# p.v of an attention layer in unsplit fp32, two key/value heads in the two column halves of TensorE

## The chip, the cores and the metric

The kernel runs on one core of one Trainium2 chip. The metric is the time of an execution on the device in microseconds; three runs of the kernel before gave a median of 988.04 us (985.65 to 988.46).

## The reference

One encoder layer is applied with shared weights to two requests: `x_prompt` of 1024 tokens and `x_sample` of 512, both 1024 wide, all in fp32. A combined projection gives a retention branch of 4 heads and an attention branch with 8 query heads of 64 columns over 2 key/value heads. The attention is bidirectional and without a mask:

```
sc  = einsum('bqkgd,bskd->bkgqs', qi, k) * scale
p   = softmax(sc, axis=-1)
out = einsum('bkgqs,bskd->bqkgd', p, v)
```

Four query heads share a key/value head. The output of each branch is gated, the branches are concatenated, and one output projection, a gate and a residual follow.

## The kernel before

The kernel runs the sample first (`sequence(1, 4, True)`, `nt` = 4 token tiles of 128) and then the prompt (`sequence(0, 8, False)`, `nt` = 8). Names of tiles end in `s` or `p` for the two. Each sequence has a part with projections and retention, and a part with the attention and the output projection, in which rows of both are mixed.

Precise products are made on TensorE from operands split into a high part, which fits fp32r, and the rest (`split`, L137): the high part by a cast on ScalarE or GpSimd, the low part by a subtraction on VectorE or GpSimd. `mm3` (L147 to L150) then takes three matmuls. A matmul of plain fp32 operands is issued once and shows in the trace as two records of weight load and two of matmul.

For a query tile t (128 queries), `nat_head` (L849) computes the scores of one query head against all keys for their maximum only (`pn`, reduced by VectorE to `nm`). `st_unit` (L900) then computes transposed scores, keys on partitions: a unit u is a head v and a pair of key blocks kp, and gives 128 keys x 512 (four query heads of 128 queries) twice in a `wide` PSUM tile `pT`. A first matmul for each block multiplies k by `Q1T`, a second one (65 rows) adds the low parts and minus the maximum, from `Q2T`, which has one buffer for each v and is filled by `mid_t` (L867). ScalarE's exp (L912) writes `p`, in fp32; `split` makes `ph` (ScalarE) and `pl` (VectorE). GpSimd adds p into `acc` (L921, L924), a slot of 512 columns for each head that all query tiles use in turn.

`pv_unit` (L926) multiplies with V. V is kept split, `VV[:, kb, v, :, :]` holding 64 columns of high part and 64 of low part, in opposite order for the two heads. With these 128 columns as weights and `ph` and `pl` as moving operands, `po` holds products with the high part in one half of its partitions and with the low part in the other; at the end of a head ScalarE copies the low half to `o` (L950) and VectorE adds the high half (L951). Units run over the key blocks of head 0 first and head 1 next, so `po` is opened and emptied twice for each query tile.

`row_sums` (L954) multiplies each head's `acc` with a 64-column block of ones, fp32, into half of the partitions of `pL`. `normalise` (L960) takes its reciprocal as exp(-ln) on ScalarE, multiplies the gate in (L969) and multiplies `o` by it (L970). `gate_out` splits the result for the output projection `out_step` (L1008), whose result `py` is scaled and added to the residual by VectorE (L1019, L1020) and stored.

PSUM has 8 banks. In the attention part of the prompt three `wide` tiles (two banks each) hold `pT`, `pn`, the transposes and `pL`, and two `bank` tiles hold `po` and `py`; in the sample there are two wide tiles and four banks.

The order is planned. Each step is put into a round with a priority by `at_round`; a tile has nt + 1 rounds, and the steps of neighbouring tiles fall into the same rounds (the maxima of the next tile, the output projection of the one before). The steps are traced in that order, and a scheduler with a simulated timeline then fixes each engine's instruction order and the buffers. On the chip an engine works its list in order. `tc.high_priority()` moves instructions ahead in the scheduler, and `add_manual_dep` adds a dependency.

Of the kernel before, what the change touches and what calls it, by code (L numbers as in the profile page):

```python
# [11 lines left out]
F32 = mybir.dt.float32  # L12
F32R = mybir.dt.float32r
BF16 = mybir.dt.bfloat16
AF = mybir.ActivationFunctionType
ALU = mybir.AluOpType
AX = mybir.AxisListType
PSUM = bass.MemoryType.PSUM

P = 128  # L20
# [18 lines left out]
KPOST = (1, 1)  # L39
PESUM = (0, 0)  # L40
EPS = 1e-6
# [37 lines left out]
def hybrid_layer_kernel(ctx: ExitStack, tc: tile.TileContext, a: dict, y_prompt: bass.AP, y_sample: bass.AP):  # L79
# [34 lines left out]
    V.memset(mhalf, -0.5)  # L114
    zo = cst.tile([P, 4, DH], F32R, name="zo")
    for i in range(4):
        V.tensor_scalar(out=zo[:, i, :], in0=ident[:, 0:DH], scalar1=0.0, scalar2=float(i == 2), op0=ALU.mult, op1=ALU.add)
    zr = zo[:, 0:2, :].rearrange("p i d -> p (i d)")
    ones = zo[:, 2, :].bitcast(F32)
    vones = [zo[:, 2 - v : 4 - v, :].rearrange("p i d -> p (i d)") for v in range(2)]  # L120

# [169 lines left out]

    def x_stats(pl, tag, x, name, sp=None):
        sp = sp or pl
        junk = pl.tile([P, D], BF16, tag=tag, name=f"junk{name}")
        ss = sp.tile([P, 1], F32, tag="xss", name=f"ss{name}", bufs=4)
        S.activation(junk, x, AF.Square, accum_out=ss)
        rr = rsqrt(sp, ss, 1, 1.0 / D, EPS, f"x{name}")
        G.tensor_scalar(out=x, in0=x, scalar1=rr, scalar2=0.0, op0=ALU.mult, op1=ALU.add)
# [16 lines left out]
    def sequence(r, nt, first):  # L315
# [4 lines left out]
        with ExitStack() as sctx:  # L320
# [18 lines left out]
            def open_kv():  # L339
                kvp = sctx.enter_context(pool(f"kv{tg}", bufs=1, reuse_waits="tile"))  # L340
                kv["k"] = [kvp.tile([P, ntok], F32R, name=f"kk{tg}{v}") for v in range(2)]
                kv["k2"] = [kvp.tile([65, ntok], F32R, name=f"k2{tg}{v}") for v in range(2)]
                kv["V"] = kvp.tile([P, nt, 2, 2, DH], F32R, name=f"VV{tg}")
                kv["g"] = kvp.tile([P, 2, DH], F32, name=f"gq{tg}")
                kv["gate"] = [kvp.tile([P, 512], F32, name=f"gate{tg}{n}") for n in range(2)] if first else gmod
# [84 lines left out]
            def kvq_units(pa):  # L430
                def kv_unit(g, tabs):
# [16 lines left out]
                    for u, pj in enumerate(pjs):  # L448
                        gs_ = slice(g * 4 + 2 * u, g * 4 + 2 * u + 2)
                        for v in range(2):  # L450
                            src = pj[:, :, P + v * DH : P + (v + 1) * DH]
                            S.copy(VV[:, gs_, v, v, :], src)
                            V.tensor_tensor(VV[:, gs_, v, 1 - v, :], src, VV[:, gs_, v, v, :].bitcast(F32), op=ALU.subtract)
                    V.tensor_tensor(t1, t1, rr.unsqueeze(2).broadcast_to([P, 8, DH]), op=ALU.mult)
# [433 lines left out]

            pesum = order[:PESUM[r]]

            def st_first(t, u):
                v, kp = u // (nt // 2), u % (nt // 2)
                hs = slice(v * 4, v * 4 + 4)
                pT = st8[t]["pT", u] = wide(f"pT{tg}{t}{u}")
                for i in range(2):
                    kb = slice((2 * kp + i) * P, (2 * kp + i + 1) * P)
                    T.matmul(pT[:, i * 512 : (i + 1) * 512], kk[v][:, kb], st8[t]["Q1T"][:, hs, :].rearrange("p h q -> p (h q)"),  # L897
                             start=True, stop=False)

            def st_unit(t, u):  # L900
                d = st8[t]
                v, kp = u // (nt // 2), u % (nt // 2)
                hs = slice(v * 4, v * 4 + 4)
                if ("pT", u) not in d:
                    st_first(t, u)
                pT = d.pop(("pT", u))
                for i in range(2):
                    kb = slice((2 * kp + i) * P, (2 * kp + i + 1) * P)
                    T.matmul(pT[:, i * 512 : (i + 1) * 512], k2[v][:, kb], d["Q2T", v],  # L909
                             start=False, stop=True)  # L910
                p = pools["at"].tile([P, 1024], F32, tag="p", name=f"p{tg}{t}{u}")
                S.activation(p, pT, AF.Exp)  # L912
                ph = pools["at"].tile([P, 1024], F32R, tag="ph", name=f"ph{tg}{t}{u}", bufs=3 if first else 2)
                pl = pools["at"].tile([P, 1024], F32R, tag="pl", name=f"pl{tg}{t}{u}", bufs=3 if first else 2)
                split(S.copy, V, ph, pl, p)
                d[u] = (ph, pl)
                acc = qs[tps[0]][:, v * 512 : (v + 1) * 512]
                if t in pesum:
                    pass
                elif kp == 0:  # L920
                    G.tensor_tensor(acc, p[:, 0:512], p[:, 512:1024], op=ALU.add)  # L921
                else:
                    for i in range(2):
                        G.tensor_tensor(acc, acc, p[:, i * 512 : (i + 1) * 512], op=ALU.add)  # L924

            def pv_unit(t, u):  # L926
                d = st8[t]
                v, kp = u // (nt // 2), u % (nt // 2)
                ph, pl = d.pop(u)
                if kp == 0:  # L930
                    d["po"] = bank(f"po{tg}{t}{v}")
                if u == 0:
                    d["o"] = pools["q2"].tile([P, 512], F32, tag="o", name=f"o{tg}{t}", bufs=3 if first else 1)
                po, o = d["po"], d["o"]
                for i in range(2):
                    kb = 2 * kp + i
                    c = slice(i * 512, (i + 1) * 512)
                    lv = VV[:, kb, v, :, :].rearrange("p a d -> p (a d)")
                    T.matmul(po, lv, ph[:, c], start=(kb == 0), stop=False)  # L939
                    T.matmul(po, lv, pl[:, c], start=False, stop=(kb == nt - 1))  # L940
                if t in pesum:
                    if u == 0:
                        d["L"] = bank(f"pL{tg}{t}")
                    for i, z in enumerate((ph, pl)):
                        for j in range(2):
                            T.matmul(d["L"], vones[v], z[:, j * 512 : (j + 1) * 512],
                                     start=(u == 0 and i + j == 0), stop=(u == nt - 1 and i + j == 2))
                if kp == nt // 2 - 1:
                    mn = slice(v * DH, (v + 1) * DH)
                    S.copy(o[mn, :], po[(1 - v) * DH : (2 - v) * DH, :])  # L950
                    V.tensor_tensor(o[mn, :], po[mn, :], o[mn, :], op=ALU.add)  # L951

            def row_sums(t):
                if t in pesum:  # L954
                    return
                pl = st8[t]["L"] = bank(f"pL{tg}{t}") if nt == 4 else wide(f"pL{tg}{t}")[:, 0:512]
                for v in range(2):
                    T.matmul(pl[v * DH : (v + 1) * DH, :], ones, qs[tps[0]][:, v * 512 : (v + 1) * 512], start=True, stop=True)  # L958

            def normalise(t):  # L960
                pl, o = st8[t]["L"], st8[t]["o"]
                with tc.issue_after(acts["ln"].ins):
                    S.activation(pl, pl, AF.Ln, scale=2.0)
                S.activation(pl, pl, AF.Exp, scale=-1.0)
                tq = slice((t % 4) * P, (t % 4 + 1) * P)
                for jj in range(2):
                    gv = gs[t // 4 * 2 + jj].rearrange("p (j q) -> p j q", j=2)[:, :, tq]
                    lv = pl[:, jj * 256 : (jj + 1) * 256].rearrange("p (j q) -> p j q", j=2)
                    V.tensor_tensor(lv, lv, gv, op=ALU.mult)  # L969
                V.tensor_tensor(o, o, pl, op=ALU.mult)  # L970

# [65 lines left out]
            for n, t in enumerate(order):  # L1037
# [4 lines left out]
                for v in range(2):  # L1042
# [3 lines left out]
                    at_round(hb + per_ - 1 if n == 0 else m, 7, lambda t=t, v=v: mid(t, v))  # L1046
                    at_round(m + 1 + (0 if first else 2 if n and v else 0), 1.5 if first and not soon or n == 0 else 3.5, lambda t=t, v=v: mid_t(t, v))
                for u in range(nt):
# [3 lines left out]
                    at_round(b + u, 3, lambda t=t, u=u: st_unit(t, u))  # L1052
                    at_round(b + u + 1, 4, lambda t=t, u=u: pv_unit(t, u))
                at_round(b + nt, 4.5, lambda t=t: row_sums(t))
# [12 lines left out]
            if first:  # L1067
# [4 lines left out]
                for t in range(NAHEAD):  # L1072
                    at_round(nt * per_ - 8 + t, 0, lambda t=t: x_load(0, t, xnext[t]))
                    at_round(nt * per_ - 5 + t, 10, lambda t=t: x_stats(pools["at"], "p", xnext[t], f"0{t}", ate))
            for j in range(8):
# [61 lines left out]
```

## Time and profile before

| | |
|---|---|
| median of 3 runs | 988.04 us (985.65 to 988.46) |
| span of the profiled execution, first to last instruction | 985.3 us |
| TensorE busy | 938.8 us, 95% |
| TensorE weight loads | 813.9 us, 83% |
| VectorE busy | 626.1 us, 64% |
| GpSimd busy | 507.7 us, 52% |
| ScalarE busy | 414.3 us, 42% |

The profiled execution has no time of its own beside its span; the median lies 2.7 us above it. In the rows, PE is TensorE's matmuls, PEld its weight loads, DVE VectorE, ACT ScalarE, POOL GpSimd; L940 is line 940 of the kernel. Matmuls overlap in their pipeline, so a row's duration is longer than the distance to the next row's start. A tile's name without its number stands for all of its kind.

### The profile page before, as it was taken

The page shows a single profiled execution, that of the slowest core. Times are in us where ns is not written, and L with a number is a line of the kernel's source. Part 1 is how long each engine was busy: PE and PEld are TensorE (multiplying, and loading weights), DVE is VectorE, ACT ScalarE, POOL GpSimd, SP SyncE. Part 2 cuts the span into 40 slices and gives each one's busy share as a digit, 9 for nine tenths or more (in the row PEclk, how much of TensorE's full clock was granted, in tenths as well). Part 3 has the DMA queues.
Part 4 walks back from the last instruction along what each step waited for, and adds up shares of the span by engine and source line. Part 5 has one row for each costly group of instructions (what it writes and reads, how often), then busy time and mean ns, then how long its engine had stood idle before and what let it go on. Part 6 is the DMA issues. An engine that isn't in the chain of part 4 may idle for free. (4 is left out here: it accounts for less than half of the span.)

```text
span 985.3 us, 15952 instructions
## 1 busy us (share of the span) xinstructions
PE 938.8 (95%) x6249; PEld 813.9 (83%) x6249; DVE 626.1 (64%) x1039; ACT 414.3 (42%) x656; POOL 507.7 (52%) x404
## 2 busy tenths in 40 slices
PE   4889998999999999999999999999979999999998
PEld 3779898987676799999999988999847776776776
DVE  2474556667886683534435243457988878978975
ACT  4252233353646652122321322241465655655562
POOL 4243544474647663122223012255899779777882
PEclk9999998999999999999999999999999999999999
DMA  9964876321911711111111112100071110111011
GB/s 274 275 191 144 269 225 218 87 78 57 382 67 44 239 50 47 41 43 44 44 35 28 26 43 70 47 7 12 1 296 68 43 44 1 44 43 45 20 43 44
DMA packets 95687, 93.02 MB, mean 94 GB/s; under 512 B 23502, under 2 KB 84858, under 8 KB 92540
## 3 DMA queue, kind: packets, MB, share of 16 engines
q1 hardware_dynamic: 92876, 77.85, 25.8%
q0 software_dynamic: 2736, 14.16, 3.6%
q8 instruction: 49, 0.80, 0.3%
q14 instruction: 26, 0.21, 0.1%
HBM read 77.30 MB, written 14.68 MB: 93 GB/s over the span
## 5 line engine op out<-in xcount | busy, mean ns | idle before, releaser
L924 POOL TENSOR_TENSOR qp<-qp,pp 128x512 f32<-128x512 f32 x96 | 159.5, 1661 | 21.3 <-ACT pp L912 15.3
L139 DVE TENSOR_TENSOR plp<-pp,php 128x1024 fp32r<-128x1024 f32 x64 | 93.6, 1464 | 19.8 <-ACT php L138 19.7
L912 ACT ACTIVATE pp<-pTp 128x1024 f32<-128x1024 f32 x64 | 65.6, 1025 | 76.8 <-PE pTp L909 40.7
L856 DVE TENSOR_REDUCE nmp<-pnp 128x1 f32<-128x1024 f32 x64 | 77.3, 1212 | 11.4 <-PE pnp L854 11.4
L138 ACT CAST php<-pp 128x1024 fp32r<-128x1024 f32 x64 | 67.2, 1051 | 16.2 <-PE pop L939 14.9
L148 PE MATMUL pvgp<-wvgp,hhp 128*128 128x256 f32 x224 | 65.1, 291 | 0.0
L148 PE MATMUL pqkp<-wqkp,hhp 128*128 128x256 f32 x224 | 64.7, 289 | 0.0
L149 PE MATMUL pvgp<-wvgp,hhp 128*128 128x256 f32 x224 | 64.4, 288 | 0.0
L150 PE MATMUL pvgp<-wvgp,hlp 128*128 128x256 f32 x224 | 63.9, 285 | 0.0
L150 PE MATMUL pqkp<-wqkp,hlp 128*128 128x256 f32 x224 | 63.7, 284 | 0.0
L149 PE MATMUL pqkp<-wqkp,hhp 128*128 128x256 f32 x224 | 63.4, 283 | 0.0
L940 PE MATMUL pop<-plp,VVp 128*128 128x512 f32 x128 | 52.1, 407 | 5.7 <-DVE plp L139 5.6
L148 PE MATMUL pyp<-wo,Mhp 128*128 128x512 f32 (+1 forms) x136 | 52.8, 389 | 1.2 <-DVE op L951 0.7
L150 PE MATMUL pyp<-wo,Mlp 128*128 128x512 f32 (+1 forms) x136 | 51.6, 382 | 0.5 <-DVE Mlp L139 0.5
L149 PE MATMUL pyp<-wo,Mhp 128*128 128x512 f32 (+1 forms) x136 | 51.9, 382 | 0.0
L639 POOL TENSOR_TENSOR sp<-rt1p,rt2p 128x512 f32<-128x512 f32 x16 | 22.5, 1405 | 56.4 <-DVE rt2p L636 56.4
L939 PE MATMUL pop<-php,VVp 128*128 128x512 f32 x128 | 51.0, 398 | 0.3 <-ACT php L138 0.3
L124 POOL TENSOR_SCALAR m_retp<-ssp 128x4 f32<-128x4 f32 x8 | 1.6, 195 | 89.6 <-DVE ssp L745 89.4
L897 PE MATMUL pTp<-Q1Tp,kkp 128*128 128x512 f32 x128 | 41.4, 404 | 3.6 <-ACT pp L912 2.9
L148 PEld LDWEIGHTS pqkp<-wqkp,hhp 128*128 128x128 f32 x224 | 43.0, 192 | 0.0
L149 PEld LDWEIGHTS pqkp<-wqkp,hhp 128*128 128x128 f32 x224 | 43.0, 192 | 0.0
L150 PEld LDWEIGHTS pqkp<-wqkp,hlp 128*128 128x128 f32 x224 | 42.9, 192 | 0.0
(465 smaller groups left out, 3120.7 us busy)
## 6 DMA issues: line engine op xcount, KB each, us to landing
wo<-wod SPq DMA_DIRECT2D x16, 1024.0 KB, 5.8
wa<-in_w_ada_dram SPq DMA_DIRECT2D x16, 512.0 KB, 6.4
wod<-woz POOLq DMA_DIRECT2D x8, 1024.0 KB, 6.0
gr<-in_w_ada_dram SPq DMA_DIRECT2D x16, 256.0 KB, 4.8
xn<-in_x_prompt_dram SPq DMA_DIRECT2D x8, 512.0 KB
xrp<-in_x_prompt_dram SPq DMA_DIRECT2D x8, 512.0 KB, 3.4
out_dram<-xrp POOLq DMA_DIRECT2D x7, 512.0 KB, 3.0
xs<-in_x_sample_dram SPq DMA_DIRECT2D x4, 512.0 KB, 6.1
```

Source lines behind the costliest of these rows:

```text
L138: hi_eng(hi, src)
L139: lo_eng.tensor_tensor(lo, src, hi.bitcast(F32), op=ALU.subtract)
L148: T.matmul(out, lh, rh, start=first, stop=False)
L149: T.matmul(out, lh, rl, start=False, stop=False)
L150: T.matmul(out, ll, rh, start=False, stop=last)
L639: G.tensor_tensor(qk, t1, t2, op=ALU.add)
L856: V.tensor_reduce(nm[:, h : h + 1], pn[:, :ntok], AX.X, ALU.max, negate=True)
L897: T.matmul(pT[:, i * 512 : (i + 1) * 512], kk[v][:, kb], st8[t]["Q1T"][:, hs, :].rearrange("p h q -> p (h q)"), start=True, stop=False)
L912: S.activation(p, pT, AF.Exp)
L924: G.tensor_tensor(acc, acc, p[:, i * 512 : (i + 1) * 512], op=ALU.add)
L939: T.matmul(po, lv, ph[:, c], start=(kb == 0), stop=False)
L940: T.matmul(po, lv, pl[:, c], start=False, stop=(kb == nt - 1))
```

## The change

V is kept once, in fp32 (`VV` of nt x 2 x 64 columns); its split goes. p is not split: `ph` and `pl` go, and `p` gets a ring of its own, 6 tiles in the sample and 8 in the prompt. The units alternate between the heads (v = u % 2, kp = u // 2). `pv_pair` comes after every second unit: for both blocks of the pair, the matmul of head 0 goes into partitions 0 to 63 of one `po` and that of head 1 into 64 to 127, in plain fp32, and head 0's waits for the exp of head 1 too. `po` is opened once for a query tile, and `normalise` multiplies straight out of it. The row sums of head 0 wait for GpSimd's last add of head 1. `mid_t` of head 1 comes two rounds earlier in the prompt.

```
-                kv["V"] = kvp.tile([P, nt, 2, 2, DH], F32R, name=f"VV{tg}")
+                kv["V"] = kvp.tile([P, nt, 2, DH], F32, name=f"VV{tg}")
...
-                        for v in range(2):
-                            src = pj[:, :, P + v * DH : P + (v + 1) * DH]
-                            S.copy(VV[:, gs_, v, v, :], src)
-                            V.tensor_tensor(VV[:, gs_, v, 1 - v, :], src, VV[:, gs_, v, v, :].bitcast(F32), op=ALU.subtract)
+                        S.copy(VV[:, gs_, :, :], pj[:, :, P : 2 * P].rearrange("p t (v d) -> p t v d", v=2))
...
-                v, kp = u // (nt // 2), u % (nt // 2)
+                v, kp = u % 2, u // 2
...
-                p = pools["at"].tile([P, 1024], F32, tag="p", name=f"p{tg}{t}{u}")
-                S.activation(p, pT, AF.Exp)
-                ph = pools["at"].tile([P, 1024], F32R, tag="ph", name=f"ph{tg}{t}{u}", bufs=3 if first else 2)
-                pl = pools["at"].tile([P, 1024], F32R, tag="pl", name=f"pl{tg}{t}{u}", bufs=3 if first else 2)
-                split(S.copy, V, ph, pl, p)
-                d[u] = (ph, pl)
+                p = d["p", u] = pools["at"].tile([P, 1024], F32, tag="p", name=f"p{tg}{t}{u}", bufs=PBUFS[r])
+                d["exp", u] = S.activation(p, pT, AF.Exp)
...
+            def pv_pair(t, kp):
                 d = st8[t]
+                ps = [d.pop(("p", 2 * kp + v)) for v in range(2)]
                 if kp == 0:
+                    d["po"] = bank(f"po{tg}{t}")
+                with tc.high_priority():
+                  for i in range(2):
+                    for v in range(2):
+                        m = T.matmul(d["po"][v * DH : (v + 1) * DH, :], VV[:, 2 * kp + i, v, :], ps[v][:, i * 512 : (i + 1) * 512],
+                                     start=(kp + i == 0), stop=(2 * kp + i == nt - 1))
+                        if v == 0:
+                            tc.add_manual_dep(m.ins, d["exp", 2 * kp + 1].ins.name, SYNC, reason="both column halves at once")
...
-                if kp == nt // 2 - 1:
-                    mn = slice(v * DH, (v + 1) * DH)
-                    S.copy(o[mn, :], po[(1 - v) * DH : (2 - v) * DH, :])
-                    V.tensor_tensor(o[mn, :], po[mn, :], o[mn, :], op=ALU.add)
...
                 for v in range(2):
-                    T.matmul(pl[v * DH : (v + 1) * DH, :], ones, qs[tps[0]][:, v * 512 : (v + 1) * 512], start=True, stop=True)
+                    m = T.matmul(pl[v * DH : (v + 1) * DH, :], ones, qs[tps[0]][:, v * 512 : (v + 1) * 512], start=True, stop=True)
+                    if v == 0:
+                        tc.add_manual_dep(m.ins, d["sum", 1].ins.name, SYNC, reason="both halves at once")
...
+                    V.tensor_tensor(lg[:, jc].rearrange("p (j q) -> p j q", j=2), pl[:, jc].rearrange("p (j q) -> p j q", j=2),
+                                    gv, op=ALU.mult)
+                V.tensor_tensor(lg, po, lg, op=ALU.mult)
...
-                    at_round(m + 1 + (0 if first else 2 if n and v else 0), 1.5 if first and not soon or n == 0 else 3.5, lambda t=t, v=v: mid_t(t, v))
+                    at_round(m + 1, 1.5 if first and not soon or n == 0 else 3.5, lambda t=t, v=v: mid_t(t, v))
...
-                    at_round(b + u + 1, 4, lambda t=t, u=u: pv_unit(t, u))
+                    if u % 2:
+                        at_round(b + u + 1, 4, lambda t=t, u=u: pv_pair(t, u // 2))
```

A path that was switched off (`PESUM`, row sums of chosen tiles on TensorE) is removed, with its table of ones.

## Rows read from the trace of the kernel before

**Rows 1.** Busy time of each engine (instructions) by stretch, granted clock, DMA share, GB/s.
```profile
core 0: us, PE busy (x) PEld busy (x) DVE busy (x) ACT busy (x) POOL busy (x), PEclk, DMA share, GB/s
215.00:333.00 118.00, 116.05 (x512) 86.88 (x512) 86.24 (x117) 61.91 (x83) 70.82 (x63) 1.00 0.41 152
...
673.00:755.00 82.00, 75.45 (x421) 60.73 (x421) 72.49 (x96) 38.98 (x45) 66.94 (x48) 0.98 0.29 113
755.00:965.00 210.00, 204.65 (x897) 153.79 (x896) 174.47 (x180) 124.81 (x140) 171.21 (x113) 1.00 0.10 33
965.00:985.30 20.30, 15.49 (x82) 11.93 (x80) 10.30 (x15) 2.59 (x5) 2.54 (x2) 1.00 0.14 52
```

**Rows 2.** TensorE's waits in 673 to 986 us: for whom, us, times, longest.
```profile
PE pop L940 <- DVE plp L139: 5.6, 6, 1.2
PE pTp L897 <- ACT pp L912: 2.9, 3, 2.1
PE pLp L958 <- POOL qp L924: 1.5, 1, 1.5
PE pyp L148 <- DVE op L951: 0.7, 1, 0.7
...
PE pyp L148 <- ACT Mhp L138: 0.4, 1, 0.4
```

**Rows 3.** Groups by line and shape: count, busy us, mean ns, idle before and releasers.
```profile
L924 POOL TENSOR_TENSOR qp<-qp,pp 128x512 f32<-128x512 f32 x96 | 159.5, 1661 | 21.3 <-ACT pp L912 15.3 <-POOL qp L924 0.4
L139 DVE TENSOR_TENSOR plp<-pp,php 128x1024 fp32r<-128x1024 f32 x64 | 93.6, 1464 | 19.8 <-ACT php L138 19.7
...
L138 ACT CAST php<-pp 128x1024 fp32r<-128x1024 f32 x64 | 67.2, 1051 | 16.2 <-PE pop L939 14.9
L912 ACT ACTIVATE pp<-pTp 128x1024 f32<-128x1024 f32 x64 | 65.6, 1025 | 76.8 <-PE pTp L909 40.7 <-DVE plp L139 14.3 <-POOL qp L924 9.0
L940 PE MATMUL pop<-plp,VVp 128*128 128x512 f32 x128 | 52.1, 407 | 5.7 <-DVE plp L139 5.6
L939 PE MATMUL pop<-php,VVp 128*128 128x512 f32 x128 | 51.0, 398 | 0.3 <-ACT php L138 0.3
...
L958 PE MATMUL pLp<-qp,zo 128*64 128x512 f32 x32 | 17.0, 647 | 1.5 <-POOL qp L924 1.5
...
L951 DVE TENSOR_TENSOR op<-pop,op 64x512 f32<-64x512 f32 x16 | 10.9, 683 | 1.8 <-ACT op L950 1.6
...
L958 PE MATMUL pLs<-qs,zo 128*64 128x512 f32 x16 | 7.5, 618 | 1.1 <-POOL qs L924 1.1
```

**Rows 4.** Timeline of TensorE, start us and duration us: both heads' row sums together.
```profile
270.60 0.40 PE L939 MATMUL pos<-phs,VVs 128*128 128x512 f32 x1
270.83 0.40 PE L940 MATMUL pos<-pls,VVs 128*128 128x512 f32 x1
271.16 1.08 PE L958 MATMUL pLs<-qs,zo 128*64 128x512 f32 x4
272.17 0.49 PE L854 MATMUL pns<-kks,Q1Ts 128*128 128x512 f32 x1
272.51 0.40 PE L872 MATMUL pq2s<-identr,Q2s 128*65 128x128 f32 x4
```

**Rows 5.** The same view: lone visits of the row sums in the prompt.
```profile
733.82 1.97 PE L958 MATMUL pLp<-qp,zo 128*64 128x512 f32 x2 [1.52 <-POOL qp L924]
...
829.87 1.07 PE L958 MATMUL pLp<-qp,zo 128*64 128x512 f32 x2
830.87 0.50 PE L148 MATMUL pyp<-wo,Mhp 128*128 128x512 f32 x1
...
835.06 1.07 PE L958 MATMUL pLp<-qp,zo 128*64 128x512 f32 x2
...
864.90 1.07 PE L958 MATMUL pLp<-qp,zo 128*64 128x512 f32 x2
```

**Rows 6.** The same view: fp32 matmuls of 128 columns in four column strips.
```profile
28.25 0.64 PE L220 MATMUL pm<-wa,scT 128*32 128x128 f32 x16 [0.43 <-DMA wa<-in_w_ada_dram]
...
33.32 1.08 PE L220 MATMUL pm<-wa,scT 128*32 128x128 f32 x32
```

More of the change, by code (lines that the diff above doesn't have):

```diff
@@ L18 @@
 PSUM = bass.MemoryType.PSUM
+SYNC = mybir.DependencyInfo(mybir.DependencyClass.Sync, mybir.DependencyReason.DATA)
 P = 128
@@ L39 @@
 KPOST = (1, 1)
-PESUM = (0, 0)
+PBUFS = (6, 8)
 EPS = 1e-6
@@ L114, in hybrid_layer_kernel @@
     V.memset(mhalf, -0.5)
-    zo = cst.tile([P, 4, DH], F32R, name="zo")
-    for i in range(4):
+    zo = cst.tile([P, 3, DH], F32R, name="zo")
+    for i in range(3):
         V.tensor_scalar(out=zo[:, i, :], in0=ident[:, 0:DH], scalar1=0.0, scalar2=float(i == 2), op0=ALU.mult, op1=ALU.add)
@@ L119, in hybrid_layer_kernel @@
     ones = zo[:, 2, :].bitcast(F32)
-    vones = [zo[:, 2 - v : 4 - v, :].rearrange("p i d -> p (i d)") for v in range(2)]
     def rsqrt(pl, ss, n, mul, add, name):
@@ L290, in x_load, with x_stats @@
         nc.sync.dma_start(x, xs[r][t * P : (t + 1) * P, :])
-    def x_stats(pl, tag, x, name, sp=None):
+    def x_stats(pl, tag, x, name, sp=None, bufs=None):
         sp = sp or pl
-        junk = pl.tile([P, D], BF16, tag=tag, name=f"junk{name}")
+        junk = pl.tile([P, D], BF16, tag=tag, name=f"junk{name}", **({"bufs": bufs} if bufs else {}))
         ss = sp.tile([P, 1], F32, tag="xss", name=f"ss{name}", bufs=4)
@@ L887, in read_wo @@
                 nc.sync.dma_start(pools["wo"][n][:, k : k + 2, :, :].bitcast(F32), wod[n][:, k : k + 2, :, :])
-            pesum = order[:PESUM[r]]
             def st_first(t, u):
-                v, kp = u // (nt // 2), u % (nt // 2)
+                v, kp = u % 2, u // 2
                 hs = slice(v * 4, v * 4 + 4)
@@ L901, in st_unit @@
                 d = st8[t]
-                v, kp = u // (nt // 2), u % (nt // 2)
-                hs = slice(v * 4, v * 4 + 4)
+                v, kp = u % 2, u // 2
                 if ("pT", u) not in d:
@@ L917, in st_unit @@
+                d["exp", u] = S.activation(p, pT, AF.Exp)
                 acc = qs[tps[0]][:, v * 512 : (v + 1) * 512]
[L918 to L921, printed above, removed]
+                if kp == 0:
+                    d["sum", v] = G.tensor_tensor(acc, p[:, 0:512], p[:, 512:1024], op=ALU.add)
                 else:
                     for i in range(2):
-                        G.tensor_tensor(acc, acc, p[:, i * 512 : (i + 1) * 512], op=ALU.add)
@@ L926, in pv_unit @@
-            def pv_unit(t, u):
+                        d["sum", v] = G.tensor_tensor(acc, acc, p[:, i * 512 : (i + 1) * 512], op=ALU.add)
+            def pv_pair(t, kp):
                 d = st8[t]
-                v, kp = u // (nt // 2), u % (nt // 2)
-                ph, pl = d.pop(u)
+                ps = [d.pop(("p", 2 * kp + v)) for v in range(2)]
                 if kp == 0:
[L931 to L947, printed above, removed]
-                if kp == nt // 2 - 1:
-                    mn = slice(v * DH, (v + 1) * DH)
-                    S.copy(o[mn, :], po[(1 - v) * DH : (2 - v) * DH, :])
-                    V.tensor_tensor(o[mn, :], po[mn, :], o[mn, :], op=ALU.add)
@@ L953, in row_sums @@
             def row_sums(t):
-                if t in pesum:
-                    return
-                pl = st8[t]["L"] = bank(f"pL{tg}{t}") if nt == 4 else wide(f"pL{tg}{t}")[:, 0:512]
+                d = st8[t]
+                pl = d["L"] = bank(f"pL{tg}{t}") if nt == 4 else wide(f"pL{tg}{t}")[:, 0:512]
                 for v in range(2):
-                    T.matmul(pl[v * DH : (v + 1) * DH, :], ones, qs[tps[0]][:, v * 512 : (v + 1) * 512], start=True, stop=True)
+                    m = T.matmul(pl[v * DH : (v + 1) * DH, :], ones, qs[tps[0]][:, v * 512 : (v + 1) * 512], start=True, stop=True)
+                    if v == 0:
+                        tc.add_manual_dep(m.ins, d["sum", 1].ins.name, SYNC, reason="both halves at once")
@@ L960, in normalise @@
             def normalise(t):
-                pl, o = st8[t]["L"], st8[t]["o"]
+                d = st8[t]
+                pl, po = d["L"], d["po"]
+                lg = d["o"] = pools["q2"].tile([P, 512], F32, tag="o", name=f"o{tg}{t}", bufs=3 if first else 1)
                 with tc.issue_after(acts["ln"].ins):
@@ L967, in normalise @@
                     gv = gs[t // 4 * 2 + jj].rearrange("p (j q) -> p j q", j=2)[:, :, tq]
-                    lv = pl[:, jj * 256 : (jj + 1) * 256].rearrange("p (j q) -> p j q", j=2)
-                    V.tensor_tensor(lv, lv, gv, op=ALU.mult)
-                V.tensor_tensor(o, o, pl, op=ALU.mult)
+                    jc = slice(jj * 256, (jj + 1) * 256)
+                    V.tensor_tensor(lg[:, jc].rearrange("p (j q) -> p j q", j=2), pl[:, jc].rearrange("p (j q) -> p j q", j=2),
+                                    gv, op=ALU.mult)
+                V.tensor_tensor(lg, po, lg, op=ALU.mult)
             final = None if first else order[-1]
@@ L1073, in sequence @@
                     at_round(nt * per_ - 8 + t, 0, lambda t=t: x_load(0, t, xnext[t]))
-                    at_round(nt * per_ - 5 + t, 10, lambda t=t: x_stats(pools["at"], "p", xnext[t], f"0{t}", ate))
+                    at_round(nt * per_ - 5 + t, 10, lambda t=t: x_stats(pools["at"], "p", xnext[t], f"0{t}", ate, PBUFS[r]))
             for j in range(8):
```

## Prediction

> **What bounds the kernel now.** I read the stage table first. In the prompt's attention (755 to 965 us) TensorE is busy 204.65 of 210.00 us, VectorE 174.47, GpSimd 171.21, ScalarE 124.81 [rows 1]. So TensorE sets the pace, at full clock, and two others stand at more than 80%. The idle time of TensorE over the four attention stretches is 1.95 + 6.55 + 5.35 + 4.81 = 18.7 us [rows 1]: no relief of another engine can give back more than that. The rest must come from the length of TensorE's own stream.
>
> Next the waits of TensorE in the prompt's attention: 5.6 us for the low half of p (`pl`, VectorE), 2.9 us for an exp of ScalarE, 1.5 us for the row sums' adds on GpSimd, 0.7 us for `o` and 0.4 us for its split [rows 2]. The groups by line say why the exp comes late: exp is idle 14.3 us until VectorE's subtraction, the cast `ph` 14.9 us until a p.v matmul frees its buffer [rows 3]. The split is a chain ScalarE, VectorE, TensorE, and back through its buffers.
>
> Then the timeline, because a busy time of pipelined matmuls is not what they cost. Two p.v matmuls begin 0.23 us apart although each is shown 0.40 us long [rows 4]. I count costs in such steps.
>
> **p.v on TensorE.** Before, a pair of key blocks of one head is four matmuls, of both heads eight: 8 x 0.23 = 1.84 us [rows 4]. There are (128 + 128) / 8 = 32 such pairs in the prompt [rows 3] and 4 tiles x 2 in the sample, 40, so 73.6 us. After, a pair is four fp32 matmuls into 64 of the 128 output columns. The trace has this very form in the row sums: each source matmul leaves two records (32 for 16 matmuls [rows 3]), for one head alone 1.00 us from its start, 829.87, to the next matmul's start [rows 5]. Once both heads stood together: four records, 271.16 to 272.17, 1.01 us [rows 4]. Two halves cost what one costs. The visit also costs at its edges: 270.83 to 272.51 is 1.68 us, which holds two ordinary steps of 0.23, so the visit takes 1.22 us, of which some 0.34 is entry and exit [rows 4]. The second block of the pair adds two more records in each half. Their step is in the four-strip matmuls at the start: 16 records of 128 columns take 0.64 us, 32 take 1.08; 16 more, four in each strip, are 0.44 us, 0.11 per 128 columns, so 0.44 per 512 columns and 0.88 for two [rows 6]. A pair is then 1.22 + 0.88 = 2.10 us, 40 pairs 84.0 us: **+10.4 us**. Bounds: with no edges 4 x 0.44 = 1.76, 70.4 us (-3.2); with the halves in turn 1.22 + 3 x 0.88 = 3.86, 154 us (+81). I take 2.10, since its form stands in a row.
>
> That row shows the halves fully together: 1.08 us busy with four records, 1.07 with two [rows 4, 5]. The Trainium skill, "TensorE: Matmul & The Clock Gate", Part 3 ("Measured speedup vs the span model"), says that three column tiles were measured at 2.38 times one, not 3. By that share a pair would be an estimated 1.76 x 3 / 2.38 + 0.34 = 2.56 us, and the time 18 us longer. I go by the row, of this form and width; partial overlap is a rival below.
>
> **Row sums.** Before, the heads' sums are issued as they come ready, mostly apart: at 829.87 and 835.06 in one tile [rows 5]. The prompt's 17.0 us over 32 records are 14 lone visits and one of four records (13 x 1.07 + 1.97 + 1.08), the sample's 7.5 us seven visits, one of them of four [rows 3 to 5]; the 1.97 is the one at 733.82, after a wait of 1.52 us. That makes 22 visits. After, 12, one for each query tile: 10 x 1.22 = **-12.2 us**. If they should fail to pair, 0; if they stand right behind a p.v pair and share its edges, 12 x 0.34 = 4 us more. I take -12.2: the added wait makes both ready at once. TensorE's stream so changes by 10.4 - 12.2 = -1.8 us.
>
> **ScalarE and VectorE.** The casts (64 x 1.05 and 16 of the sample) and the subtractions (64 x 1.46 and 16) go, and so do the two-step moves of `po` out of PSUM. In the prompt the split is 67 us of ScalarE and 94 of VectorE [rows 3], neither of them the bound. They count by the waits that end in them: 5.6 + 2.9 + 0.7 + 0.4 [rows 2] = **-9.6 us**; the sample's are left out as small. Bounds 0 (the wait moves to the next late engine) and -18.7 (all idle time goes). I take -9.6, by the named rows. What is late next is GpSimd: its 96 adds take 1661 ns each [rows 3] and each tile's sums need all of that tile's; no row says what they take beside an idler VectorE, and I count nothing for it.
>
> **Added waits.** (a) The first p.v matmul of a pair waits for the exp of both heads. Behind it stand the scores of the next unit and the output projection's matmuls. The exp runs one round earlier, and a round is 35.03 us / 9 = 3.9 us (a tile has nine rounds, and the same visit comes at 829.87 and 864.90 [rows 5]); an exp is 1.03 us [rows 3] and ScalarE has just been freed. 0; without that cover 1.03 us for each of 40. (b) The row sums of the first head wait for GpSimd's last add of the second. Behind them on TensorE stand output projection and scores, and the next tile's first add waits for them, since one buffer holds the sums. Between 0 and the 5.2 us that now lie between the two visits [rows 5], for each tile; I take 0.2 (2 us in all), since TensorE's waits now hold 1.5 us for them in all [rows 2]. (c) With the heads alternating, head 0's second query operand (`Q2T`, one buffer for each head) is read until unit 6 instead of 3; the copy that fills it for the next tile waits on VectorE, and behind that stand the reductions of `nat_head`. It is due three rounds later. 0, up to one VectorE pass over 1024 columns (1.46 us as the subtraction's [rows 3]) per prompt tile, 12 us. (d) `po` stays in its bank until the normalisation, and the output projection has the other bank. Its two tenants follow each other anyway, and the scores use other PSUM tiles. 0, up to the 1.4 us of one eviction (two VectorE passes of 512 columns, 0.68 each as the pass on `o` [rows 3]) per prompt tile, 11 us. So **+2 us**, of 0 to 41 + 12 x 5.2 + 12 + 11 = 126.
>
> **Without effect.** Half of V's copies and all of its subtractions go from the projections, where TensorE is busy beside them; the wider ring of p tiles is SBUF alone; the query transposes moved up by two rounds for head 1 issue the same work, and no DMA moves.
>
> **Sum.** -1.8 - 9.6 + 2 = -9.4 us against the profiled execution: its span is 985.3, so 975.9. The median of the runs is 988.04, 2.7 above that span; the same 2.7 around the new span gives 978.6, forecast as 979 us.
>
> **Rivals.** (1) The idle time only moves: the stream gives -1.8, the waits nothing, +2: 988 us. For it: two engines over 80% busy [rows 1] and an order fixed ahead. Against it: the waits named go by their cause. (2) Slower, by the row sums' wait: the order puts the pair where the first head's visit stood, and TensorE's queue stands until GpSimd has ended. The price is up to 5.2 us per prompt tile, for the seven that have a successor, 36 us: 1015 us; at half of it 997. It decides from 9.4 / 7 = 1.3 us per tile beyond what I took. For it: GpSimd at 171 of 210 us, and a chain through its adds; against it: slack of 39 us there, and lighter neighbours. (3) The halves overlap in part or not at all. Midway between 2.10 and 3.86, 2.98 us per pair adds 35: 1014 us; in turn 979 + 70 + 12 x 0.88 = 1060 (then the change does not do what it says). The Trainium skill's 2.38 for three column tiles, cited above, belongs here, with an estimate of 997 us. Against it: the four-record visit in rows 4. (4) All idle time goes: -1.8 - 18.7 = -20.5, 967.5 us. For it: the granted clock is 0.98 in 673 to 755 us [rows 1], after waits that may go too.
>
> **Chances.** Forecast 0.55, (1) 0.13, (2) 0.13, (3) 0.05, (4) 0.14. About 0.3% (3 us) is what a measurement here tells from no change. Slower holds (2), (3) and a little of (1), 0.19; same is the rest of (1) and the weak end of the forecast, 0.13; faster 0.68. The forecast's own range is 971 to 985. The range takes in (4), (1) and (2) to half its price: 965 to 997.
>
> **What would show it.** Right: p.v records in bundles of eight, about 2.1 us from the first to the next full-width matmul; 12 row-sum visits of about 1.0 us; VectorE down by some 130 us (80 x 1.46 and 24 x 0.68), ScalarE by 95 (80 x 1.05 and the moves of `po`); no wait of TensorE for a subtraction; the tile spacing down from 35 to about 34 us. Wrong: bundles of 3.5 us or more (3); a wait of 2 us or more before each row-sum visit (2); output projection's first matmuls waiting for the normalisation (d); a spacing still at 35 with the same idle time (1).

## The result, and the profile after

The changed kernel takes 995.61 us (median of 4 runs, 994.19 to 996.42) where the kernel before takes 987.83 (985.65 to 988.46): a ratio of 1.0079, interval 1.0064 to 1.0094. It is 0.8% slower, where 979 was forecast. The time lies inside the range of 965 to 997, on the other side of no change.

First the page's busy times of the changed kernel, whose span is 994.5 us. Before, VectorE was busy 626.1 us, ScalarE 414.3, GpSimd 507.7.

```profile
PE 935.0 (94%) x6249; PEld 775.4 (78%) x6249; DVE 493.6 (50%) x922; ACT 320.2 (32%) x546; POOL 439.6 (44%) x404
```

VectorE and ScalarE gave back what they were meant to, 132 and 94 us. GpSimd, for which nothing was counted, gave back 68. Only the end came later. The stage table of the changed kernel says where (columns as in [rows 1]).

```profile
215.00:333.00 118.00, 115.55 (x534) 81.16 (x533) 60.01 (x98) 43.98 (x62) 61.62 (x65) 1.00 0.43 155
...
755.00:965.00 210.00, 188.74 (x831) 117.39 (x828) 94.21 (x115) 67.44 (x77) 121.53 (x105) 1.00 0.09 30
965.00:994.50 29.50, 23.97 (x117) 16.76 (x115) 6.26 (x12) 2.95 (x5) 7.46 (x7) 0.92 0.10 36
```

In the prompt's attention TensorE stands idle for 21.3 of 210 us, where it was 5.35 [rows 1], at the same clock. And it stands idle although every other engine is less loaded than before: VectorE is at 94 us instead of 174. The sample and the prompt went different ways. The next rows are TensorE's first weight load for transposing the prompt's rows and the start of its last matmul, first before and then after:

```profile
333.31 1.02 PEld L508 LDWEIGHTS xTp<-identr,xn 128*128 128x128 f32 x8
981.31 0.28 PE L150 MATMUL pyp<-wo,Mlp 128*128 128x256 f32 x1
```

```profile
329.90 0.59 PEld L505 LDWEIGHTS xTp<-identr,xn 128*128 128x128 f32 x4
990.53 0.28 PE L150 MATMUL pyp<-wo,Mlp 128*128 128x256 f32 x1
```

The prompt starts at 329.9 us instead of 333.3. From there to the last matmul it is 660.6 us instead of 648.0. So the sample gained 3 us and the prompt lost 12 to 13.

TensorE's waits in 673 to 996 us of the changed kernel, in the columns of [rows 2]:

```profile
PE pop L922 <- ACT pp L906: 8.9, 8, 1.2
PE pLp L931 <- POOL qp L912: 7.4, 7, 2.3
PE pnp L851 <- ACT Q1Tp L841: 5.5, 5, 1.1
PE pnp L851 <- DVE nmp L853: 2.5, 5, 0.5
PE pyp L148 <- DVE op L948: 1.8, 1, 1.8
PE pTp L892 <- DVE Q2Tp L871: 1.1, 2, 0.8
PE pTp L892 <- ACT pp L906: 0.7, 1, 0.7
```

The waits of [rows 2] for the low half of p are gone. Others stand in their place, 27.9 us in these seven rows. The first four come five to eight times each, and the prompt has eight tiles: these are waits of the turn from one query tile to the next. The next view shows one turn: TensorE's timeline in the changed kernel, from the last matmuls before it. A bracket holds the idle time just before, and what ended it.

```profile
829.39 0.40 PE L148 MATMUL pyp<-wo,Mhp 128*128 128x512 f32 x1
...
831.92 0.40 PE L150 MATMUL pyp<-wo,Mlp 128*128 128x512 f32 x1
832.15 0.62 PE L892 MATMUL pTp<-Q1Tp,kkp 128*128 128x512 f32 x2
832.61 0.62 PE L903 MATMUL pTp<-Q2Tp,k2p 65*128 65x512 f32 x2
834.40 1.94 PE L922 MATMUL pop<-pp,VVp 128*64 128x512 f32 x8 [1.17 <-ACT pp L906]
837.10 1.08 PE L931 MATMUL pLp<-qp,zo 128*64 128x512 f32 x4 [0.75 <-POOL qp L912]
838.11 0.87 PE L838 MATMUL pq1p<-identr,Q1p 128*128 128x128 f32 x8
840.07 0.73 PE L851 MATMUL pnp<-kkp,Q1Tp 128*128 128x512 f32 x2 [1.10 <-ACT Q1Tp L841]
...
842.48 0.73 PE L851 MATMUL pnp<-kkp,Q1Tp 128*128 128x512 f32 x2 [0.50 <-DVE nmp L853]
...
874.12 1.08 PE L931 MATMUL pLp<-qp,zo 128*64 128x512 f32 x4 [0.75 <-POOL qp L912]
```

The turn is a chain that goes back and forth between engines: the last scores, their exp, the last p.v bundle, GpSimd's two adds, the row sums, the transposes of the query of a later tile, ScalarE's cast of them, the maxima of the new tile, VectorE's reduction. Where the four waits stand, nothing else is placed in TensorE's list, and it is idle for 1.17 + 0.75 + 1.10 + 0.50 = 3.52 us. The row sums come every 874.12 - 837.10 = 37.02 us, where tiles were 35.03 apart [rows 5].

The kernel before has the same chain at its turn, but fills it. Its timeline from the first head's row sums (the row at 829.87 in [rows 5]) to the second's (835.06):

```profile
831.67 0.39 PE L940 MATMUL pop<-plp,VVp 128*128 128x512 f32 x1
...
832.84 0.40 PE L149 MATMUL pyp<-wo,Mhp 128*128 128x512 f32 x1
833.07 0.54 PE L841 MATMUL pq1p<-identr,Q1p 128*128 128x128 f32 x5
833.45 0.47 PE L940 MATMUL pop<-plp,VVp 128*128 128x512 f32 x1
...
834.22 0.38 PE L841 MATMUL pq1p<-identr,Q1p 128*128 128x128 f32 x3
...
```

Here single p.v matmuls, single matmuls of the output projection and the transposes alternate: 8, 6 and 8 of them between the two row sums, and no bracket shows idle time. This kernel too issues most of its output matmuls ahead of the last scores; much of the filler is p.v itself. After the change the p.v is one bundle of eight records that is issued once both exps have ended. The 12 matmuls of the output projection that are ready early (columns `k` 0 to 3, at 829.39 to 831.92 above) run ahead of the last scores, not behind them.

### The profile page after: what moved, and what is told of

Its sections match the earlier page's. It is cut to its first block, busy times and chain, and to the rows that moved or that the text cites. A ratio compares the mean times of both kernels' runs of the same rounds, so it can differ in the third digit from the quotient of the medians.

```text
span 994.5 us, 15648 instructions
## 1 busy us (share of the span) xinstructions
PE 935.0 (94%) x6249; PEld 775.4 (78%) x6249; DVE 493.6 (50%) x922; ACT 320.2 (32%) x546; POOL 439.6 (44%) x404
## 5 line engine op out<-in xcount | busy, mean ns | idle before, releaser
L912 POOL TENSOR_TENSOR qp<-qp,pp 128x512 f32<-128x512 f32 x96 | 125.9, 1320 | 63.7 <-ACT pp L906 61.1
L922 PE MATMUL pop<-pp,VVp 128*64 128x512 f32 x256 | 62.0, 605 | 8.9 <-ACT pp L906 8.9
L851 PE MATMUL pnp<-kkp,Q1Tp 128*128 128x512 f32 x128 | 41.9, 413 | 8.0 <-ACT Q1Tp L841 5.5
L922 PEld LDWEIGHTS pop<-pp,VVp 128*64 128x64 f32 x256 | 15.5, 136 | 38.9 <-issue 24.0
L148 PEld LDWEIGHTS pvgp<-wvgp,hhp 128*128 128x128 f32 x224 | 42.8, 191 | 0.0
L149 PEld LDWEIGHTS pvgp<-wvgp,hhp 128*128 128x128 f32 x224 | 42.8, 191 | 0.0
```

What stands on the lines that cost most here:

```text
L148: T.matmul(out, lh, rh, start=first, stop=False)
L149: T.matmul(out, lh, rl, start=False, stop=False)
L851: T.matmul(pn[:, c], Q1T[:, h, :], kk[v][:, c], start=True, stop=True)
L912: d["sum", v] = G.tensor_tensor(acc, acc, p[:, i * 512 : (i + 1) * 512], op=ALU.add)
L922: m = T.matmul(d["po"][v * DH : (v + 1) * DH, :], VV[:, 2 * kp + i, v, :], ps[v][:, i * 512 : (i + 1) * 512], start=(kp + i == 0), stop=(2 ...
```

## The experiments

Two edits lie in the change that could bare the turn: the row sums' wait for both heads (rival 2), and `high_priority`, by which the scheduler puts p.v ahead of the scores and leaves the output projection to be used up early. "Prompt starts" below is the weight load shown above, at 333.3 and 329.9 us, and "spacing" the distance of the row sums of two tiles, as 37.02 above. Each run's ratio is to executions of the kernel before that were timed beside it; starts, lengths and spacings are of one profiled execution each.

### The row sums' wait alone, and without it

e1 takes the wait out of the changed kernel:

```diff
-                    if v == 0:
-                        tc.add_manual_dep(m.ins, d["sum", 1].ins.name, SYNC, reason="both halves at once")
```

> The changed kernel without the added wait of the row sums: head 0's may go before head 1's adds have ended. Theory A (the paired row sums gate the turn from one query tile to the next: last exp, two adds on GpSimd, row sums, Q1 transposes, ScalarE's Q1T, next maxima, with TensorE idle in between): the tile spacing falls from 37.0 to 35 to 36 us although 12 more visits of 0.9 to 1.2 us are paid; median 983 to 991. Theory B (the p.v bundle of eight records, which needs both exps, has taken away the small matmuls that filled TensorE's gaps): the spacing stays at 37 or grows by the extra visit; median 994 to 1004.

991.23 us, ratio 1.0040 (1.0025 to 1.0055); spacing 35.25 to 35.86. The prompt starts at 337.0 and takes 649.8 us. So the wait helps the sample by 7 us and costs the prompt 11. It does not explain the whole loss: without it the kernel is still slower than before. e2 puts the wait, with no other edit, into the kernel before:

```diff
                 for v in range(2):
-                    T.matmul(pl[v * DH : (v + 1) * DH, :], ones, ...)
+                    m = T.matmul(pl[v * DH : (v + 1) * DH, :], ones, ...)
+                    if v == 0:
+                        tc.add_manual_dep(m.ins, st8[t]["sum", 1].ins.name, SYNC, ...)
```

> The kernel before with that one wait alone: head 0's row sums wait for the last add of head 1, p.v stays split. A: the 10 visits saved (12 us) are eaten by the turn; the spacing does not fall below 35 us, median 986 to 996. B: the visits saved come through: spacing 34 us, median 976 to 982.

1008.25 us, ratio 1.0213 (1.0180 to 1.0246), worse than either kernel and than what was expected. Two rows of this kernel, a wait of TensorE in 673 to 1001 us and one of ScalarE:

```profile
PE pLp L959 <- POOL qp L925: 8.0, 5, 3.4
```

```profile
ACT pp L913 <- POOL qp L925: 22.1, 15, 2.4
```

The row sums wait 8.0 us, up to 3.4 at a time; and exp, which waited 9.0 us for the adds to free a p tile [rows 3], waits 22.1. This prices the wait in the kernel before, with its two p tiles and slower adds; how much of it is in the changed kernel is e1's to say.

### p.v's priority

e3 takes the priority from the changed kernel and leaves the rest:

```diff
-                with tc.high_priority():
+                if True:
```

> The changed kernel with p.v not moved ahead in the scheduler. A: the turn is the same, 993 to 998. B: p.v can lie where TensorE would be idle; 984 to 990.

983.59 us, ratio 0.9971 (0.9950 to 0.9992): 12 us below the changed kernel, and now just faster than before. Its turn on TensorE:

```profile
826.58 0.62 PE L892 MATMUL pTp<-Q1Tp,kkp 128*128 128x512 f32 x2
827.04 0.63 PE L903 MATMUL pTp<-Q2Tp,k2p 65*128 65x512 f32 x2
827.51 0.39 PE L148 MATMUL pyp<-wo,Mhp 128*128 128x512 f32 x1
...
830.05 0.39 PE L150 MATMUL pyp<-wo,Mlp 128*128 128x512 f32 x1
830.37 1.94 PE L922 MATMUL pop<-pp,VVp 128*64 128x512 f32 x8
832.13 1.03 PE L931 MATMUL pLp<-qp,zo 128*64 128x512 f32 x4
833.09 0.87 PE L838 MATMUL pq1p<-identr,Q1p 128*128 128x128 f32 x8
835.06 0.74 PE L851 MATMUL pnp<-kkp,Q1Tp 128*128 128x512 f32 x2 [1.10 <-ACT Q1Tp L841]
...
866.91 1.03 PE L931 MATMUL pLp<-qp,zo 128*64 128x512 f32 x4
```

The same 12 matmuls now stand between the last scores and the bundle. The exp and the adds run beside them, the waits of 1.17 and 0.75 are gone from this turn, and that of 1.10 for the cast is left (so is that of 0.50 behind it). The spacing is 34.78 us. e11 makes both edits of e1 and e3:

> The changed kernel with neither the added wait of the row sums nor p.v moved ahead: fp32 p.v in the two column halves alone. If each of the two did harm only through the turn, which the 12 output matmuls now cover, this comes near to the run without priority with its extra lone visits paid: 983 to 989. If the row sums' wait was still a cost of its own without priority, it is faster than that run: 976 to 982.

985.19 us, ratio 0.9964 (0.9950 to 0.9977). With it the two edits make a table, prompt's start and then the prompt's length in us (before: 333.3 and 648.0):

```
                        p.v with priority     without
row sums wait for both  329.9, 660.6 (after)  332.2, 646.2 (e3)
row sums as ready       337.0, 649.8 (e1)     339.4, 641.6 (e11)
```

The wait gains 7 us in the sample in both columns. In the prompt it costs 10.8 us with the priority and 4.6 without. The priority costs the prompt 14.4 with the wait and 8.2 without, and seems to gain 2.3 to 2.4 us in the sample. So neither edit alone is the cause: both bare the turn in the prompt, and together they cost more than one by one (19.0 against 8.2 + 4.6 = 12.8).

How far one execution each can be trusted, the kernels that follow tell. The prompt's length repeats: it is 660.9 us in e8, whose prompt differs from the changed kernel's in one order alone, and 646.3 in e6, whose prompt is that of e3. The start does not: eight kernels with one and the same sample part (the changed one, e4 to e7, e9, e10 and e12) start the prompt at 327.7 to 332.1 us. The 7 us of the wait stand clear of that, the 2.3 of the priority do not. Over whole runs the priority costs 1.1% with the wait (1.0079 against 0.9971) and 0.8% without (1.0040 against 0.9964).

### Is it the filler?

e5 keeps the priority, and lets the prompt's 12 matmuls of the output projection be issued only behind the last scores:

```diff
-                    T.matmul(pT[:, i * 512 : (i + 1) * 512], k2[v][:, kb], d["Q2T", v],
+                    d["st"] = T.matmul(pT[:, i * 512 : (i + 1) * 512], k2[v][:, kb], d["Q2T", v],
...
-                mm3(d["py"], ...)
+                with tc.issue_after(d["st"].ins) if u < 4 and not first else ExitStack():
+                    mm3(d["py"], ...)
```

> The changed kernel, p.v still moved ahead, with one edge more in the prompt: the output projection's matmuls over the retention columns (12 of each query tile, 2.8 us, ready long before) may not be issued before that tile's last scores. Theory C (moving p.v ahead lets these 12 be spent before the last scores, so that at the turn TensorE has nothing to do while exp, GpSimd's adds and Q1T come): the wait for exp falls from 8.9 to under 2 us, the spacing from 37.0 to 35 us, median 982 to 987. Theory D (it is the place of p.v ahead of the scores itself that delays the chain): spacing 36 to 37 us, median 990 to 996.

987.48 us, ratio 0.9982 (0.9969 to 0.9994), some 8 us below the changed kernel, between what the two theories expected; spacing 36.07. TensorE's waits in 673 to 996 us of this kernel:

```profile
PE pnp L851 <- ACT Q1Tp L841: 5.5, 5, 1.1
PE pLp L931 <- POOL qp L912: 4.1, 5, 2.3
...
PE pop L922 <- ACT pp L906: 1.8, 2, 1.2
```

The wait for exp falls from 8.9 to 1.8 us, that of the row sums from 7.4 to 4.1, the cast's stays. So the place of the filler is a cause, with no other edit of the order. Of the 37.02 - 34.78 = 2.24 us per tile between the changed kernel and e3 it explains 0.95. Of the other 1.29, the traces show 0.45 as a wait of the row sums and 0.31 as a wait for `Q2T` that stand in e5's tiles and not in e3's; the rest, some 0.5, goes with the priority in a way that no run takes apart.

e4 asks whether covering another link would do. It issues the query's transposes ahead of the row sums:

```diff
-                    at_round(hb - (4 if n == 1 else 1), 8, lambda t=t: nat_prep(t))
+                    at_round(hb - (4 if n == 1 else 1), 8 if first or n == 1 else 4.2, lambda t=t: nat_prep(t))
```

> The changed kernel with the Q1 transposes of the next tile but one traced ahead of the row sums in the same round of the prompt. A: TensorE's wait for Q1T (5.5 us in the prompt) goes and half of that for the adds is filled: 986 to 991. B: the wait only moves, 993 to 997.

997.49 us, ratio 1.0110 (1.0078 to 1.0141). The wait for the cast is gone, and the row sums' wait has doubled:

```profile
PE pLp L931 <- POOL qp L912: 15.1, 7, 4.5
```

At this bare turn, the work moved ahead of one wait only lengthened another. e6 drops the priority in the prompt alone, where it costs, and keeps it in the sample; e7 is e6 with e4's edit:

```diff
-                with tc.high_priority():
+                with tc.high_priority() if first else ExitStack():
```

> The changed kernel with p.v moved ahead in the sample alone. The sample stage should end as in the changed kernel (prompt starts at 330 us against 332 without any priority) and the prompt should run as without priority (spacing 34.8 us): median 980 to 983 by C and D both.

> The same as the run with p.v moved ahead in the sample alone, and with the Q1 transposes traced ahead of the row sums in the prompt. C: with the 12 matmuls at the turn as cover, the wait for Q1T (5.5 us) goes and does not come back at the row sums: spacing 33.8 to 34.3 us, median 974 to 979. If Q1's place only hands the wait on to the row sums, as it did with p.v moved ahead: 980 to 985.

e6: 981.57 us, 0.9935 (0.9913 to 0.9958), prompt's start 330.2, spacing 34.79, as the two cells of the table say. e7: 979.71 us, 0.9901 (0.9878 to 0.9924), spacing 33.63. The same edit that gained nothing in e4 gives 1.16 us a tile where the turn is covered (the ratios of e6 and e7 overlap; the spacing tells them apart). In e7's timeline the transposes stand ahead of the bundle, and these rows hold no idle time; 0.72 us follow behind them, for a reduction and an exp:

```profile
827.62 0.39 PE L150 MATMUL pyp<-wo,Mlp 128*128 128x512 f32 x1
827.85 0.81 PE L838 MATMUL pq1p<-identr,Q1p 128*128 128x128 f32 x8
828.59 1.94 PE L922 MATMUL pop<-pp,VVp 128*64 128x512 f32 x8
830.36 1.03 PE L931 MATMUL pLp<-qp,zo 128*64 128x512 f32 x4
831.32 0.73 PE L851 MATMUL pnp<-kkp,Q1Tp 128*128 128x512 f32 x2
```

### Do the column halves need to alternate?

e8 is the changed kernel with its two loops swapped, so that head 0's p.v is issued whole and then head 1's:

```diff
-                  for i in range(2):
-                    for v in range(2):
+                  for v in range(2):
+                    for i in range(2):
```

> The changed kernel with the four matmuls of a p.v pair issued head by head: both blocks of head 0, then both of head 1, instead of alternating; nothing else moves at the turn. If a half can only start in the order of issue, the halves overlap at the seam alone: a bundle takes 3.0 to 3.5 us instead of 1.87, 40 bundles add 45 to 66 us, median 1040 to 1062. If the column halves run from queues of their own, 1.9 us and 994 to 998.

994.53 us, ratio 1.0071 (1.0054 to 1.0089), as the changed kernel. The bundle takes the same time. First the changed kernel's rows, then e8's:

```profile
848.16 0.39 PE L150 MATMUL pyp<-wo,Mlp 128*128 128x512 f32 x1
848.47 1.94 PE L922 MATMUL pop<-pp,VVp 128*64 128x512 f32 x8
850.34 0.73 PE L851 MATMUL pnp<-kkp,Q1Tp 128*128 128x512 f32 x2
```

```profile
846.33 0.39 PE L150 MATMUL pyp<-wo,Mlp 128*128 128x512 f32 x1
846.65 1.95 PE L922 MATMUL pop<-pp,VVp 128*64 128x512 f32 x8
848.52 0.73 PE L851 MATMUL pnp<-kkp,Q1Tp 128*128 128x512 f32 x2
```

850.34 - 848.47 = 1.87 us, and 848.52 - 846.65 = 1.87 us. The halves run side by side in both orders.

### What the wait is worth once the turn is covered

e9 is e7 without the row sums' wait in the prompt (`if v == 0 and first:`), e10 is e7 with the prompt's row sums and normalisation one round later (`late` is true for every prompt tile but the last):

```diff
-                at_round(b + nt, 4.5, lambda t=t: row_sums(t))
-                at_round(b + nt + (1 if first and n == 0 else 0), 8.5, lambda t=t: normalise(t))
+                at_round(b + nt + late, 2.5 if late else 4.5, lambda t=t: row_sums(t))
+                at_round(b + nt + (late or n == 0), 2.6 if late else 8.5, lambda t=t: normalise(t))
```

> The run without priority and with Q1 ahead, and in the prompt without the added wait of the row sums. If the wait has cost nothing since the turn is covered, only the lone visits are left, 7 to 8 more of 0.9 to 1.2 us: 985 to 989. If it still holds up TensorE: 974 to 981.

> The run without priority and with Q1 ahead, with the paired row sums and the normalisation of all prompt tiles but the last traced one round later, so that the 12 output matmuls stand between p.v and the sums. The wait for the adds (7.7 us, 5.8 of it in the first tile) goes: 970 to 976. If the next tile's adds, which must wait for the sums, get late in turn: 979 to 984.

e9: 980.41 us, 0.9922 (0.9902 to 0.9942), no difference from e7 (979.71) that the intervals tell. Inside it there is one. Counted from the prompt's start, the row sums of the second tile are issued in full 4.0 us earlier than in e7 (763.48 - 332.11 against 763.04 - 327.70), and each later tile takes 34.73 instead of 33.63. e10: 982.73 us, 0.9952 (0.9936 to 0.9968), spacing 34.66. The row sums still wait 5.2 us, in one place, and the wait for exp, 1.1 us in e7, is back with 3.9: the 12 matmuls now stand behind the bundle (827.86 to 830.53 us at one turn), no longer in front of it. e12 takes what e9 showed, and drops the wait for the first prompt tile alone:

```diff
-                    if v == 0:
+                    if v == 0 and (first or t != order[0]):
```

> The best run so far (no priority in the prompt, Q1 transposes ahead of the row sums) with the row sums' wait taken off the first query tile of the prompt alone, where TensorE waits 5.8 us for GpSimd's adds. If that wait is the pairing's, it goes at the price of one lone visit: 972 to 977. If GpSimd is late there by itself (it also adds the rotary terms of the remaining queries), the second head's sums wait as long: 978 to 982.

975.26 us (973.19 to 977.15), ratio 0.9866 (0.9844 to 0.9888), the fastest here and below both kernels; its interval just overlaps e7's. Spacing 33.63. Its stage row, and two of its waits in 673 to 996 us, of which the first was 7.7 us in e7, 5.8 of them at one place:

```profile
755.00:965.00 210.00, 201.27 (x908) 128.95 (x907) 92.75 (x120) 70.20 (x80) 124.96 (x110) 1.00 0.09 31
```

```profile
PE pLp L931 <- POOL qp L912: 4.5, 2, 2.5
...
PE pop L922 <- ACT pp L906: 1.1, 2, 0.5
```

## Why the prediction was wrong

The spans give the account in one line: 994.5 - 985.3 = +9.2 us, of which TensorE's busy time is -3.8 (938.8 to 935.0) and its idle time +13.0. The forecast was -1.8 for the stream and -9.6 + 2 = -7.6 for the idle time. The work was sized nearly right; the waits were not.

**p.v's length: right.** It was put at 2.10 us a pair. From the first record to the next full-width matmul it is 1.87; the step into it is 848.47 - 848.16 = 0.31 where 0.23 is ordinary, and the step behind it is part of the next matmul, shown 0.73 for two where a plain pair is 0.62 (832.15 above). That gives an estimate of 1.87 + 0.08 + 0.11 = 2.06 us, 40 of them 82.4 where 84.0 was forecast. Rival 3, halves that overlap in part, is refuted by these bundles and by e8. In turn, eight records of 0.44 us would take an estimated 3.5 us, so two halves were 3.5 / 1.87 = 1.9 times as fast. The Trainium skill's 2.38 for three column tiles ("TensorE: Matmul & The Clock Gate", Part 3, "Measured speedup vs the span model") has no counterpart in these runs.

**Row sums: right in size.** They stand in visits of four records, 838.11 - 837.10 = 1.01 us, one for each tile. The stream did become shorter; it is seen at last in e7 and e12, whose tiles are 33.63 us apart, 1.4 less than 35.03. Over two tiles (829.87 to 899.92 us before, 830.36 to 897.64 in e7) TensorE's busy time is 67.59 and 65.84 us, its idle time 2.46 and 1.44: of the 1.4, some 0.9 is the stream and 0.5 idle time.

**ScalarE and VectorE: the relief right, what it is worth wrong.** 132 and 94 us less were forecast as 130 and 95, and the waits of [rows 2] went. But the -9.6 us were read as net.

**Added waits: the step that failed.** It took 2 us and got 16 more of idle time in the prompt's attention alone (21.3 against 5.35). Term (a) was put at 0 since "the exp runs one round earlier". That holds inside a tile and not at its turn, where the scores of the last pair, its exp and its p.v follow each other with nothing between; the price there, 1.17 us, is close to the 1.03 named for the case without cover. The text even listed what stands behind the p.v, but not that the priority would have used up the work that could stand before it. Term (b) took 0.2 us a tile; at this turn it is 0.75, in all seven waits 7.4, in e4 15.1. Two further waits of the turn, for the cast of `Q1T` and the first reduction, 8.0 us, were not in the sum at all. Terms (c) and (d) were rightly small: 1.1 us, and 1.8 in one place.

**Rivals.** Rival 2 had the side, one of the places and, at half its price, nearly the time (997). That closeness, and that 995.61 lies in the stated range, is luck: the rival blamed the row sums' wait alone, and by the table the priority costs more in the prompt, 14.4 us against 10.8, the wait gives 7 back in the sample, and e1 is slower than before without it. Rival 1 had the idle time move; it moved and grew. Rival 4, that all of it goes, is out. The clock explains little: it was 1.00 in 755 to 965 us in both kernels. In the last stretch it was 0.92 against 1.00 before, and from the last row sums to the last matmul's start it was 13.07 us (977.46 to 990.53) against 12.71 (968.60 to 981.31).

**Not settled.** Why the scheduler places the 12 matmuls where it does was read from the issued order, not from its costs. Some 0.5 of the 1.29 us a tile that e5 leaves, and how the wait saves 7 us in the sample, were not taken apart. The change's other edits (alternating units, the ring of p, the earlier `mid_t`) were never taken out one by one; with both the priority and the wait out (e11) the kernel is 0.4% below the one before, where 0.9% was forecast.

## What to carry to other kernels

The idle time of the bounding engine caps what relief can give, but says nothing of what a new order can lose; so walk the tile boundary separately, list the dependent chain there link by link, and name for each link the independent instructions that lie behind it in the issued order. Merging many small matmuls into one bundle that waits for everything takes away filler as well as work, and a priority for that bundle may use up the filler that is left before it is needed. When a change that shortens the stream comes out slower, put its order edits back one at a time, together and by stage: here the same arithmetic went from 0.8% slower to 1.3% faster.

## What the hardware showed unasked

The two column halves overlap whatever the issue order: 1.87 us with head 0's four records issued ahead of head 1's (e8), the same as alternating. Were records started in the order of issue, head 1's first would come no earlier than head 0's second matmul, 0.88 us in, and with its own four records of 0.44 the bundle would take an estimated 2.6 us at least. So across the column halves, "an engine works its list in order" does not hold for when records start.

GpSimd's adds of 128x512 became faster without being touched. Their group in the changed kernel, against 1661 ns in [rows 3]:

```profile
L912 POOL TENSOR_TENSOR qp<-qp,pp 128x512 f32<-128x512 f32 x96 | 125.9, 1320 | 63.7 <-ACT pp L906 61.1
```

Before, VectorE was busy 174 of 210 us beside them [rows 1], after 94. Before's own trace narrows it down: the 62 adds that overlap a subtraction of p on VectorE (L139) took 1859 ns on average, the 34 others 1301, about what all of them take after the change. So slow adds go with that subtraction rather than with VectorE's load as such; no run here takes the subtraction out alone.
